# Attention of an encoder kernel: two heads at a time, scores issued alternately, transposes cut into two 64-row halves

## The chip, the core and the metric

The kernel runs on one core of one Trainium2 chip. The metric is the device time of one execution in microseconds (us). TensorE (PE) multiplies 128-row tiles and loads the stationary tile in a separate step (PEld); VectorE (DVE), ScalarE (ACT) and GpSimd (POOL) do the elementwise work; SyncE (SP) issues the transfers. PE writes to PSUM, which has eight banks; the kernel hands them out in turn.

## The reference

Two layers of an encoder over 256 tokens of width 1024, batch 1, in fp32. The change touches the attentions only:

```
q = rms_norm(...); k = rms_norm(...)          # per head, 256 tokens
s = einsum('bqhd,bkhd->bhqk', q, k) * scale   # (+ bias, + sink logit, by group)
p = softmax_f32(s)
o = einsum('bhqk,bkhv->bqhv', p, v)
```

Each layer has a first FFN, a mixer with 16 heads (8 latent heads with keys of 96 numbers; 4 windowed and 4 neighbourhood heads with keys of 64 numbers and a bias), an output projection, a cross-attention with 4 heads of 64 to 256 memory tokens, and a second FFN.

## The kernel before

Tokens lie in two tiles of 128 rows (t = 0, 1). Weights come in tiles of 128x1024, are split on ACT and DVE into a high and a low fp32r part (`whi`, `wlo`), and each product is three matmuls (`mm3`: L167, L168, L169). The FFNs are a long unbroken row of these.

A head of an attention goes through four steps. **Scores** (L438): for each t one fp32 matmul, queries stationary (64 or 96 rows, 128 columns), keys moving (256 columns); the profile shows each fp32 matmul as two passes, so a head's scores are four records. The windowed, neighbourhood and memory heads have 64-number keys: of the two heads of a `Pair`, head 0 lies in partitions 0 to 63 and head 1 in 64 to 127 of the same tile. **Softmax**: maximum on DVE (L441 for latent and memory heads, L447 with the bias for the others), exponentials on ACT (L454). **Transposes** (L465): four 128x128 blocks of the weights `p` into one PSUM bank, p stationary, an identity `ident` moving, then two copies to `pT` on DVE (L467, L468). **Values** (L474): four matmuls, `pT` stationary, V moving with 65 columns, again two passes each. When both heads of a pair are through, `finish` divides (L416, L418).

`attend` writes the heads in order: step i emits the scores of head i, the transposes of head i - d1 and the values of head i - d2. Queries and keys of the latent heads are turned one head ahead (`prep_latent`, L794, L795, 96 columns stationary, copied by ACT at L797, L798), those of the neighbourhood heads by `prep_blocks` (L739). Between the heads hooks emit other PE work: the memory keys (`mem.keys`, matmuls into `kvk`), the normed groups' transposes (L864). A scheduler then orders each engine's queue by its own estimate of times, so the written order is not kept exactly. Names: `mx0` is the mixer of layer 0, `me0` its memory attention; `sw`, `na`, `ml` are windowed, neighbourhood and latent pairs, a digit for the pair and one for the head (`mx0na01sc` holds the scores of head 1 of pair 0); `sc`, `pt`, `pv`, `qt` are the PSUM tiles of scores, turned weights, values and turned queries and keys.

## Time and profile before

| | |
|---|---|
| median of three runs | 1053.08 us (1052.95 to 1059.89) |
| the profiled execution | 1048.1 us, of which its instructions span 1046.3 us |
| PE busy | 1024.0 us, 98% |
| PE loading weights | 1002.4 us, 96% |
| DVE, ACT busy | 718.0 us (69%), 556.7 us (53%) |
| granted clock of PE | 0.996 of its upper level of 2.4 GHz |

Matmuls overlap in the profile, since each record holds the latency of its end: the time that a matmul takes from its neighbours is the distance between starts, not its duration. The two mixers' attentions lie at about 236 to 288 us and 752 to 805 us, the two memory attentions at about 321 to 332 us and 837 to 848 us.

### The profile page before, as it was taken

To read this page: it belongs to the slowest core of one execution; us is meant where nothing else is said; L and a number is where in the kernel's file an instruction comes from. 1 tells how busy PE (TensorE), PEld (TensorE's weight loads), DVE (VectorE), ACT (ScalarE), POOL (GpSimd) and SP (SyncE) were. 2 spreads that over 40 slices of the span, in tenths; PEclk is the share of its full clock that TensorE was granted. 3 is DMA by queue.
4 is the path that set the end of the run, shared out by engine and by line. 5 is a ranking of instruction groups with operands and counts; after the bars stand their busy time and mean duration, and the time that the engine had idled before them with its cause. 6 is when DMAs were issued, how large, how long until landed. Compare 5 with 4: busy or idle time off the path is not lost.

```text
span 1046.3 us, 20916 instructions
## 1 busy us (share of the span) xinstructions
PE 1024.0 (98%) x8480; PEld 1002.4 (96%) x8480; DVE 718.0 (69%) x1249; ACT 556.7 (53%) x928; POOL 114.2 (11%) x107
## 2 busy tenths in 40 slices
PE   8999999999999999999999999999999999999996
PEld 7999999998998999999999999999889999999996
DVE  7866667778786676666757666667886777766652
ACT  5755455566563565555545444546675546554541
POOL 4000000072031400000000000002600313000000
PEclk9999999999999999999999999999999999999998
DMA  8866666655042655555555555655531517666641
GB/s 277 276 208 192 198 199 206 186 173 182 22 136 67 234 189 199 188 199 192 192 184 187 188 186 184 206 186 167 181 131 32 172 38 241 204 189 196 194 130 41
DMA packets 54529, 181.79 MB, mean 174 GB/s; under 512 B 6048, under 2 KB 8992, under 8 KB 54432
## 3 DMA queue, kind: packets, MB, share of 16 engines
q1 hardware_dynamic: 54432, 180.45, 54.2%
q8 instruction: 66, 1.08, 0.4%
q14 instruction: 31, 0.25, 0.1%
HBM read 179.38 MB, written 1.05 MB: 172 GB/s over the span
## 4 chain that ended last, share of the span: by engine, by line
PE 72%; issue 17%; DVE 4%; POOL 2%; DMA 2%; ACT 2%; SPq 0%; POOLq 0%; DVEq 0%; ACTq 0%
PE f11i L169 4%; PE f11i L167 4%; PE f11i L168 4%; PE f01i L169 3%; PE f01i L167 3%; PE f01i L168 3%; PE f02i L168 3%; PE f02i L167 3%; PE f02i L169 3%; PE f11o L169 2%; PE f11o L167 2%; PE f11o L168 2%; PE f02o L169 2%; PE f01o L169 2%; PE f02o L168 2%
## 5 line engine op out<-in xcount | busy, mean ns | idle before, releaser
L141 DVE TENSOR_TENSOR wlo<-raw,whi 128x1024 fp32r<-128x1024 f32 (+4 forms) x337 | 407.5, 1214 | 208.9 <-ACT whi L140 207.7
L140 ACT CAST whi<-raw 128x1024 fp32r<-128x1024 f32 (+4 forms) x337 | 343.8, 1024 | 345.1 <-issue 86.0
L167 PE MATMUL f11i<-n10h,whi 128*128 128x256 f32 x320 | 90.1, 282 | 0.0
L168 PE MATMUL f11i<-n10l,whi 128*128 128x256 f32 x320 | 89.8, 281 | 0.0
L169 PE MATMUL f11i<-n10h,wlo 128*128 128x256 f32 x320 | 89.8, 281 | 0.0
L167 PE MATMUL f02i<-n20h,whi 128*128 128x256 f32 x320 | 88.5, 277 | 0.0
L167 PE MATMUL f01i<-n0h,whi 128*128 128x256 f32 x320 | 88.5, 277 | 0.0
L167 PE MATMUL f12i<-n21h,whi 128*128 128x256 f32 x320 | 88.5, 277 | 0.0
L169 PE MATMUL f01i<-n0h,wlo 128*128 128x256 f32 x320 | 88.4, 276 | 0.0
L168 PE MATMUL f02i<-n20l,whi 128*128 128x256 f32 x320 | 88.3, 276 | 0.0
L168 PE MATMUL f12i<-n21l,whi 128*128 128x256 f32 x320 | 88.3, 276 | 0.0
L169 PE MATMUL f02i<-n20h,wlo 128*128 128x256 f32 x320 | 88.3, 276 | 0.0
L168 PE MATMUL f01i<-n0l,whi 128*128 128x256 f32 x320 | 88.3, 276 | 0.0
L169 PE MATMUL f12i<-n21h,wlo 128*128 128x256 f32 x320 | 88.3, 276 | 0.0
L168 PEld LDWEIGHTS f11i<-n10l,whi 128*128 128x128 f32 x320 | 61.4, 192 | 0.0
L168 PEld LDWEIGHTS f12i<-n21l,whi 128*128 128x128 f32 x320 | 60.1, 188 | 0.0
L168 PEld LDWEIGHTS f02i<-n20l,whi 128*128 128x128 f32 x320 | 60.1, 188 | 0.0
L168 PEld LDWEIGHTS f01i<-n0l,whi 128*128 128x128 f32 x320 | 60.1, 188 | 0.0
L167 PEld LDWEIGHTS f01i<-n0h,whi 128*128 128x128 f32 x320 | 60.1, 188 | 0.0
L167 PEld LDWEIGHTS f11i<-n10h,whi 128*128 128x128 f32 x320 | 60.1, 188 | 0.0
L169 PEld LDWEIGHTS f01i<-n0h,wlo 128*128 128x128 f32 x320 | 60.1, 188 | 0.0
L167 PEld LDWEIGHTS f02i<-n20h,whi 128*128 128x128 f32 x320 | 60.1, 188 | 0.0
(1026 smaller groups left out, 2940.4 us busy)
## 6 DMA issues: line engine op xcount, KB each, us to landing
raw<-in_w SPq DMA_DIRECT2D x311, 512.0 KB, 4.2
raw<-in_w SPq DMA_DIRECT2D x12, 384.0 KB, 3.7
raw<-in_w SPq DMA_DIRECT2D x8, 416.0 KB, 3.3
kv0mt<-in_mem SPq DMA_DIRECT2D x8, 128.0 KB, 4.3
kv1mt<-in_mem SPq DMA_DIRECT2D x8, 128.0 KB, 3.7
gx<-in_gx SPq DMA_DIRECT2D x3, 256.0 KB, 7.2
out<-gx SPq DMA_DIRECT2D x3, 256.0 KB, 2.8
gx<-in_gx SPq DMA_DIRECT2D x1, 323.0 KB, 3.2
```

Of the source, the lines that this page charges most:

```text
L140: ins = nc.scalar.copy(hi[:, a:b], r[:, a:b])
L141: nc.vector.tensor_tensor(lo[:, a:b], r[:, a:b], hi[:, a:b].bitcast(F32), ALU.subtract)
L167: nc.tensor.matmul(ps, ah, bh, start=first, stop=False)
L168: nc.tensor.matmul(ps, ah, bl, start=False, stop=False)
L169: return nc.tensor.matmul(ps, al, bh, start=False, stop=last)
```

## The change

`attend` now steps over pairs: step i turns the latent queries of the next pair, emits the scores of pair i with the two heads alternating over t, the values of pair i - 2, a hook, and the transposes of pair i - 1. Every transpose that goes through the new `turn` (weights of all heads, queries and keys of the latent and memory heads, memory keys) is cut: rows 0 to 63 of the source go to one PSUM bank and rows 64 to 127 to another, with a 64x64 corner of the identity moving, so that one 128-row transpose becomes two with 64 moving columns. The copies out of PSUM take 64 columns of four blocks each; their number and size stay. The biased scores are written in place into `p`. The hooks stand in a new order.

```
-AT = dict(
-    d1=3, d2=5, look=3, norm1=9, turn1=11, norm2=12, turn2=14, turn0=20,
-    keys=2, ksteps=3, knorm=3, kturn=13, v0=0, v1=13, e1=2, e2=4, wturn0=7, wturn1=6,
-)
+AT = dict(look=3, turn0=20, v0=0, v1=13, wturn1=6)
...
+    halves = (slice(0, 64), slice(64, 128))
+
+    def turn(nm, blocks):
+
+
+        n = int(np.prod(blocks[0].shape[1:]))
+        ps = [acc(f"{nm}{i}") for i in range(2)]
+        for b, src in enumerate(blocks):
+            for q, r in zip(ps, halves):
+                state["turned"] = nc.tensor.transpose(q[0:n, 64 * b : 64 * b + 64], src[r], ident[r, r])
+        return ps
+
     class Pair:
 
 
-        def __init__(self, nm, o, cols):
-            self.nm, self.o, self.cols = nm, o, cols
-            self.pv, self.es = None, [None, None]
-
-        def out(self, c):
-            if self.pv is None:
-                self.pv = acc(self.nm + "pv")[:, 0:260].rearrange("p (t c d) -> p t c d", t=2, c=2)
-            return self.pv[:, :, c, :]
+
+        def __init__(self, nm, o, cols, heads):
+            self.nm, self.o, self.cols, self.heads = nm, o, cols, heads
+            self.es = [None, None]
+            for c, h in enumerate(heads):
+                h.pair, h.c, h.nm = self, c, f"{nm}{c}"
+
+        def scores(self):
+            for h in self.heads:
+                h.sc = acc(h.nm + "sc").rearrange("p (t k) -> p t k", t=2)
+            for t in range(2):
+                for h in self.heads:
+                    nc.tensor.matmul(h.sc[:, t, :], h.qT[:, t * P : (t + 1) * P], h.kT, start=True, stop=True)
+            for h in self.heads:
+                h.weights()
+
+        def transposes(self):
+            ps = turn(self.nm + "pt", [
+                h.p[:, t, kt * P : (kt + 1) * P] for h in self.heads for kt in range(2) for t in range(2)
+            ])
+            for c, h in enumerate(self.heads):
+                h.pT = tp.tile([P, 2, T], F32, tag="b2", bufs=8, name=h.nm + "pT")
+                for i, r in enumerate(halves):
+                    nc.vector.tensor_copy(
+                        h.pT.rearrange("p k (t u) -> p (k t) u", t=2)[:, :, r],
+                        ps[i][:, c * T : (c + 1) * T].rearrange("p (k u) -> p k u", k=4),
+                    )
+
+        def values(self):
+            self.pv = acc(self.nm + "pv")[:, 0:260].rearrange("p (t c d) -> p t c d", t=2, c=2)
+            for h in self.heads:
+                for t in range(2):
+                    for kt in range(2):
+                        nc.tensor.matmul(
+                            self.pv[:, t, h.c, :], h.pT[:, kt, t * P : (t + 1) * P], h.V[:, kt, h.vh, :],
+                            start=kt == 0, stop=kt == 1,
+                        )
+            self.finish()
...
-                src = tp.tile([P, 2, T], F32, tag="b2", bufs=8, name=nm + "sb")
+                src = self.p
...
-        def transposes(self):
-            ps = acc(self.nm + "pt")
-            for kt in range(2):
-                for t in range(2):
-                    o = (kt * 2 + t) * P
-                    nc.tensor.transpose(ps[:, o : o + P], self.p[:, t, kt * P : (kt + 1) * P], ident)
-            self.pT = tp.tile([P, 2, T], F32, tag="b2", bufs=8, name=self.nm + "pT")
-            nc.vector.tensor_copy(self.pT[:, 0, :], ps[:, 0:T])
-            nc.vector.tensor_copy(self.pT[:, 1, :], ps[:, T : 2 * T])
-
-        def values(self):
-            pv = self.pair.out(self.c)
-            for t in range(2):
-                for kt in range(2):
-                    nc.tensor.matmul(
-                        pv[:, t, :], self.pT[:, kt, t * P : (t + 1) * P], self.V[:, kt, self.vh, :],
-                        start=kt == 0, stop=kt == 1,
-                    )
-            if self.c == 1:
-                self.pair.finish()
-
-    def attend(heads, hooks={}, d1=AT["d1"], d2=AT["d2"]):
-
-        n = len(heads)
-        heads[0].prep()
-        for i in range(n + d2):
-            if i + 1 < n:
-                heads[i + 1].prep()
+    def attend(pairs, preps={}, hooks={}):
+
+        n = len(pairs)
+        for i in range(n + 2):
+            if i in preps:
+                preps[i]()
             if i < n:
-                heads[i].scores()
-                if i + 3 < n:
-                    heads[i + 3].load()
-            if 0 <= i - d1 < n:
-                heads[i - d1].transposes()
-            if 0 <= i - d2 < n:
-                heads[i - d2].values()
-            for h in hooks.get(i, ()):
+                pairs[i].scores()
+                for p in pairs[i + 1 : i + 3]:
+                    for h in p.heads:
+                        if h not in loaded:
+                            loaded.append(h)
+                            h.load()
+            if i >= 2:
+                pairs[i - 2].values()
+            for h in hooks.get((i, 0), ()):
                 h()
+            if 1 <= i <= n:
+                pairs[i - 1].transposes()
+            for h in hooks.get((i, 1), ()):
+                h()
+
+    loaded = []
...
-            pt = acc(self.nm + "pt")
-            for b in range(2):
-                for t in range(2):
-                    o = (b * 2 + t) * P
-                    nc.tensor.transpose(pt[:, o : o + P], self.kn[:, t, 2 * b : 2 * b + 2, :], ident)
+            ps = turn(self.nm + "pt", [self.kn[:, t, 2 * b : 2 * b + 2, :] for b in range(2) for t in range(2)])
...
-        def prep_latent(h):
+        def prep_latent(pr):
+
             if not big:
                 big["q"] = slot([P, 8, T], F32, nm + "qT")
                 big["k"] = slot([P, 8, T], F32, nm + "kT")
-            ps = acc(f"{nm}qt{h}")
-            for t in range(2):
-                nc.tensor.transpose(ps[0:96, t * P : (t + 1) * P], qn[:, t, h, :], ident)
-                nc.tensor.transpose(ps[0:96, T + t * P : T + (t + 1) * P], kn[:, t, h, :], ident)
-            q, k = big["q"][0:96, h, :], big["k"][0:96, h, :]
-            nc.scalar.activation(q, ps[0:96, 0:T], AF.Copy, scale=gq[0:96, 0:1])
-            nc.scalar.activation(k, ps[0:96, T : 2 * T], AF.Copy, scale=gn[0:96, l, G_HEAD + 1 : G_HEAD + 2])
-            heads[8 + h].qT, heads[8 + h].kT = q, k
+            hs = slice(2 * pr, 2 * pr + 2)
+            ps = turn(f"{nm}qt{pr}", [
+                a[:, t, h, :] for a in (qn, kn) for h in (2 * pr, 2 * pr + 1) for t in range(2)
+            ])
+            for i, r in enumerate(halves):
+                for a, (b, g_) in enumerate((("q", gq[0:96, 0:1]), ("k", gn[0:96, l, G_HEAD + 1 : G_HEAD + 2]))):
+                    nc.scalar.activation(
+                        big[b][0:96, hs, :].rearrange("p h (t u) -> p (h t) u", t=2)[:, :, r],
+                        ps[i][0:96, a * T : (a + 1) * T].rearrange("p (k u) -> p k u", k=4), AF.Copy, scale=g_,
+                    )
+            for h in (2 * pr, 2 * pr + 1):
+                latent[h].qT, latent[h].kT = big["q"][0:96, h, :], big["k"][0:96, h, :]
...
+        preps = {1: lambda: prep_blocks(3, 5), 2: lambda: prep_blocks(4, 6)}
+        for pr in range(4):
+            preps[3 + pr] = lambda pr=pr: prep_latent(pr)
+        attend(pairs, preps, {
+            (0, 0): [lambda: mem.keys(4)], (1, 0): [lambda: mem.keys(6)], (2, 0): [lambda: mem.keys(3)],
+            (3, 0): [lambda: mem.keys(3), mem.keys_normed], (6, 1): [mem.keys_transposed],
+            (4, 0): [lambda: group_norm(1)], (5, 1): [lambda: group_transposed(1)],
+            (6, 0): [lambda: group_norm(2)], (7, 1): [lambda: group_transposed(2)],
+        })
...
-        heads = []
-        for b in range(2):
-            pair = Pair(f"{nm}a{b}", o, [2 * b, 2 * b + 1])
-            for c in range(2):
-                s = slice(64 * c, 64 * c + 64)
-                heads.append(Head(pair, c, qT[s, b, :], memkT[s, b, :], memV, 2 * b + c))
+        pairs = [
+            Pair(f"{nm}a{b}", o, [2 * b, 2 * b + 1], [
+                Head(qT[r, b, :], memkT[r, b, :], memV, 2 * b + c) for c, r in enumerate(halves)
+            ])
+            for b in range(2)
+        ]
         oh = tp.tile([P, 2, T], F32R, tag="b2", bufs=8, name=nm + "oh")
...
-        attend(heads, {AT["wturn0"]: [lambda: out_transposed(0)]}, AT["e1"], AT["e2"])
+        attend(pairs, {}, {(2, 1): [lambda: out_transposed(0)]})
```

On PE in the mixer of layer 0, the end of the first windowed pair's transposes and the scores of the first neighbourhood pair; before:

```order
L465 MATMUL mx0sw00pt<-ident,mx0sw00p 128x128 x4
L438 MATMUL mx0na00sc<-mx0sT 128x256 x2
L465 MATMUL mx0sw01pt<-ident,mx0sw01p 128x128 x4
L167 MATMUL kv0kvk_3197<-whi_2985,kv0h 128x256
L168 MATMUL kv0kvk_3197<-wlo_2986,kv0h 128x256
L169 MATMUL kv0kvk_3197<-whi_2985,kv0l 128x256
L739 MATMUL mx0st_3201<-ident,mx0qk 128x128 x4
L438 MATMUL mx0na01sc<-mx0sT 128x256 x2
```

The same place in the changed kernel (3172 and 3173 are the two banks of the halves):

```order
L401 MATMUL mx0sw0pt_3172<-ident,mx0sw01p 128x64
L401 MATMUL mx0sw0pt_3173<-ident,mx0sw01p 128x64
L419 MATMUL mx0na00sc<-mx0sT 128x256
L419 MATMUL mx0na01sc<-mx0sT 128x256
L419 MATMUL mx0na00sc<-mx0sT 128x256
L419 MATMUL mx0na01sc<-mx0sT 128x256
L164 MATMUL kv0kvk_3165<-whi_2985,kv0h 128x256
```

The two heads' scores now stand next to each other, and directly behind 64-row transposes.

On PE in the same mixer, the transposes of the first latent pair; before, those of its head 1:

```order
L438 MATMUL mx0ml20sc<-mx0kT,mx0qT 128x256 x2
L474 MATMUL mx0na1pv<-mx0V,mx0na11pT 128x65
L465 MATMUL mx0ml01pt<-ident,mx0ml01p 128x128 x4
L474 MATMUL mx0na1pv<-mx0V,mx0na11pT 128x65 x3
L794 MATMUL mx0qt_3514<-ident,mx0qn 96x128
```

After:

```order
L440 MATMUL mx0na1pv<-mx0V,mx0na10pT 128x65 x4
L401 MATMUL mx0ml0pt_3516<-ident,mx0ml00p 128x64 x4
L401 MATMUL mx0ml0pt_3516<-ident,mx0ml01p 128x64 x3
L401 MATMUL mx0ml0pt_3517<-ident,mx0ml00p 128x64
L440 MATMUL mx0na1pv<-mx0V,mx0na11pT 128x65 x4
L401 MATMUL mx0ml0pt_3517<-ident,mx0ml00p 128x64 x3
L401 MATMUL mx0ml0pt_3517<-ident,mx0ml01p 128x64 x3
L401 MATMUL mx0ml0pt_3516<-ident,mx0ml01p 128x64
L401 MATMUL mx0ml0pt_3517<-ident,mx0ml01p 128x64
L875 MATMUL mx0ot_3542<-ident,mx0o 128x128
```

Here seven halves of the lower rows stand in a row, then a 128-row values product, then seven of the upper rows.

On DVE in the memory attention of layer 0, from the last maximum on; before:

```order
L441 TENSOR_REDUCE me0a11ng<-me0a11sc 128x2
L467 COPY me0a00pT<-me0a00pt 128x256
L468 COPY me0a00pT<-me0a00pt 128x256
L467 COPY me0a01pT<-me0a01pt 128x256
L468 COPY me0a01pT<-me0a01pt 128x256
L467 COPY me0a10pT<-me0a10pt 128x256
L468 COPY me0a10pT<-me0a10pt 128x256
L467 COPY me0a11pT<-me0a11pt 128x256
L468 COPY me0a11pT<-me0a11pt 128x256
L416 RECIPROCAL me0a0rc<-me0a0pv 128x4
```

After:

```order
L476 TENSOR_REDUCE me0a11ng<-me0a11sc 128x2
L430 COPY me0a00pT<-me0a0pt_4285 128x4x64
L430 COPY me0a00pT<-me0a0pt_4286 128x4x64
L430 COPY me0a01pT<-me0a0pt_4285 128x4x64
L430 COPY me0a01pT<-me0a0pt_4286 128x4x64
L455 RECIPROCAL me0a0rc<-me0a0pv 128x4
L457 TENSOR_TENSOR me0o<-me0a0pv,me0a0rc 128x2x64 x2
L430 COPY me0a10pT<-me0a1pt_4322 128x4x64
L430 COPY me0a10pT<-me0a1pt_4323 128x4x64
```

The division of pair 0, which needs its values from PE, now stands ahead of pair 1's copies.

## Rows read from the trace of the kernel before

**Rows 1.** The page, busy time of PE: time, share of the span, instructions.
```profile
PE 1024.0 (98%) x8480; PEld 1002.4 (96%) x8480; DVE 718.0 (69%) x1249; ACT 556.7 (53%) x928; POOL 114.2 (11%) x107
```

**Rows 2.** Stretches: length, busy time of each engine, granted clock, DMA.
```profile
236.00:288.00 52.00, 51.47 (x395) 46.84 (x394) 41.16 (x136) 32.06 (x80) 6.19 (x6) 1.00 0.31 102
321.00:332.00 11.00, 10.05 (x76) 8.63 (x76) 7.41 (x20) 3.99 (x10) 0.00 (x0) 1.00 0.00 1
752.00:805.00 53.00, 53.00 (x405) 48.35 (x404) 42.04 (x136) 33.57 (x81) 4.47 (x6) 1.00 0.26 85
```

**Rows 3.** Timeline of PE, a 64-row head alone: start us, duration us, what.
```profile
246.33 0.60 PE L739 MATMUL mx0st<-ident,mx0qk 128*128 128x128 f32 x4
246.86 1.13 PE L438 MATMUL mx0na01sc<-mx0sT 64*128 64x256 f32 x4
247.92 0.39 PE L167 MATMUL kv0kvk<-whi,kv0h 128*128 128x256 f32 x1
248.15 0.28 PE L168 MATMUL kv0kvk<-wlo,kv0h 128*128 128x256 f32 x1
```

**Rows 4.** Timeline of PE, a head's values; a 96-row head and what follows.
```profile
252.25 1.00 PE L474 MATMUL mx0sw0pv<-mx0V,mx0sw01pT 128*128 128x65 f32 x8
...
260.32 1.03 PE L438 MATMUL mx0ml01sc<-mx0kT,mx0qT 96*128 96x256 f32 x4
261.18 0.60 PE L465 MATMUL mx0na10pt<-ident,mx0na10p 128*128 128x128 f32 x4
```

**Rows 5.** Timeline of PE, three 64-row heads in a row.
```profile
236.29 0.48 PE L438 MATMUL mx0sw00sc<-mx0sT 64*128 64x256 f32 x1
236.31 0.48 PE L438 MATMUL mx0sw01sc<-mx0sT 64*128 64x256 f32 x1
236.61 0.38 PE L438 MATMUL mx0sw00sc<-mx0sT 64*128 64x256 f32 x1
236.63 0.38 PE L438 MATMUL mx0sw01sc<-mx0sT 64*128 64x256 f32 x1
...
237.26 1.02 PE L438 MATMUL mx0sw10sc<-mx0sT 64*128 64x256 f32 x4
238.22 0.61 PE L251 MATMUL kv0ps<-cmean,kv0s 128*128 128x1 f32 x4
```

**Rows 6.** Timeline of PE's weight loads at the same place.
```profile
236.29 0.18 PEld L438 LDWEIGHTS mx0sw00sc<-mx0sT 64*128 64x128 f32 x1 [0.25 <-issue]
236.31 0.18 PEld L438 LDWEIGHTS mx0sw01sc<-mx0sT 64*128 64x128 f32 x1
236.40 0.19 PEld L438 LDWEIGHTS mx0sw00sc<-mx0sT 64*128 64x128 f32 x1
```

**Rows 7.** Lines L739, L794, L474: duration ns min/median/max, first and last start, forms.
```profile
L739 PE MATMUL mx0st<-ident,mx0qk x8: 270/272/273, 239.8 to 246.7; 128*128 128x128 f32 x8
L739 PEld LDWEIGHTS mx0st<-ident,mx0qk x6: 138/140/140, 239.9 to 246.6; 128*128 128x128 f32 x6
...
L794 PEld LDWEIGHTS mx0qt<-ident,mx0qn x2: 123/124/125, 257.2 to 257.4; 128*96 128x96 f32 x2
...
L474 PEld LDWEIGHTS mx0sw0pv<-mx0V,mx0sw00pT x8: 188/192/192, 249.6 to 250.4; 128*128 128x128 f32 x8
L474 PE MATMUL mx0sw0pv<-mx0V,mx0sw00pT x8: 219/275/275, 249.8 to 250.5; 128*128 128x65 f32 x8
```

**Rows 8.** Timelines of DVE, ACT and PE in the memory attention of layer 0.
```profile
322.43 0.69 DVE L441 TENSOR_REDUCE me0a00ng<-me0a00sc 128x2 f32<-128x512 f32 x1 [1.07 <-PE me0a01sc L438]
325.71 0.41 DVE L467 COPY me0a00pT<-me0a00pt 128x256 f32<-128x256 f32 x1
328.89 0.49 DVE L418 TENSOR_TENSOR me0o<-me0a0pv,me0a0rc 128x128 f32<-128x128 f32 x2
...
323.15 0.84 ACT L454 ACTIVATE me0a00p<-me0a00sc,me0a00ng 128x256 f32<-128x256 f32 x2 [1.31 <-DVE me0a00ng L441]
...
331.10 0.97 PE L167 MATMUL me0wo<-me0oh,whi 128*128 128x256 f32 x6 [0.52 <-ACT me0oh L931]
```

89 lines of the change are left out of this document (33 added, 56 removed).

## Prediction, made before the changed kernel had run

> **What bounds the kernel now.** I read the busy times first: PE is busy for 1024.0 of 1046.3 us [rows 1], so time is won only where PE's queue gets shorter or a gap in it closes. The stretches come next: in the mixers' attentions PE is busy almost throughout, 51.47 of 52.00 us in layer 0, while DVE has 41.16 and ACT 32.06; the memory attention is 11.00 us with 10.05 busy [rows 2]. So the mixers' attentions are priced by starts on PE, the memory attentions by a chain through DVE and ACT. The rest of the kernel keeps its order and costs nothing here. The change reaches about 52 + 53 + 2 x 11 = 127 us; one per cent of the total would be 8% of that.
>
> **Part A: scores side by side.** A 96-row head starts at 260.32 and what follows at 261.18: four passes in 0.86 us, 0.215 each [rows 4]. At the start of the mixer the order put three 64-row heads in a row. There the records of heads 0 and 1 start 0.02 us apart and advance together, 0.22 per round, and the third head starts at 237.26: two heads in the time of one [rows 5]. So two heads in different halves of the rows run at the same time when they stand together. Before, that holds for the first windowed pair and the first memory pair only. After, by the order, it holds also for the second windowed and first neighbourhood pair of each layer and the second neighbourhood pair of layer 1 (in layer 0 two matmuls of memory keys stand between its heads): five mixer pairs, 5 x 0.86 = **-4.3 us**. The latent heads have 96 rows; alternating them changes nothing.
>
> **Part B: going to 64 rows and back.** A 64-row head alone costs more than its passes. The transposes ahead have 0.109 between starts ((0.60 - 0.272)/3 [rows 3, 7]), so theirs end at 246.77; the scores start at 246.86, a gap of 0.09. The next row starts 1.06 later, 0.20 more than the 0.86 of a 96-row head. That row lasts 0.39 where the next one of its kind lasts 0.28: another 0.11, a load that nothing hid [rows 3, 4]. Together 0.40 us for each excursion into 64 rows. The three heads in a row show the same once for all: 1.93 us between 236.29 and 238.22, against two rounds of 0.86 [rows 5]. Now every turned tile is 64-row work among 128-row work. Counting stretches of 64-row work in the two orders: the mixers have 12 before, 37 after (19 and 18), since keys, values and latent scores stand between, and some tiles are cut into two or three stretches. For transposes I take 0.36, the load at the entry being shorter (Part C): 37 x 0.36 - 12 x 0.40 = **+8.5 us**. This is no longer hidden anywhere: PE waits for itself.
>
> **Part C: the halves.** A block of 128 rows costs 0.109 now. Its matmul lasts 272 ns with 128 moving columns; the values' lasts 219 with 65 (the shortest): 0.84 ns a column, so 64 columns are 0.054 us. Its load lasts 140 ns with 128 columns and 124 with 96, about 0.5 ns a column: 0.064 us or less for 128 [rows 7]. The loads of two heads in different halves of the rows start together too: 236.29 and 236.31, the second one of head 0 already at 236.40 [rows 6]. So a pair of halves, running side by side, should take about 0.060 in place of 0.109. The two mixers have 2 x (64 weights + 32 queries and keys + 4 memory keys) = 200 blocks: 200 x 0.049 = -9.8. But the order puts halves of one bank in a row and a values product between them in the first three latent pairs: 14, 13 and 10 slots of 0.060 where 8 would do, 2 x 13 x 0.060 = +1.6. Sum **-8.2 us**.
>
> The Trainium skill speaks against this part: "TensorE: Matmul & The Clock Gate", section "LDWEIGHTS (loading the stationary operand)", gives a load as columns over 1.2 GHz, whatever the rows. By that a half would load as long as a whole block, 0.107 us, and Part C would give nothing. The rows contradict it for transposes: their loads are 52 ns shorter than the 192 of the values' loads with the same 128 columns.
>
> **Part D: new waits in the mixers.** Pairs are coarser than heads, but between a pair's scores and its transposes there lies a whole step, some 7 us of PE, against 0.69 + 0.84 us a head on DVE and ACT. The narrow place is the end: the values of the third latent pair follow its transposes after four output transposes, while DVE has first to finish pair 1 and then make two copies of 0.41 [rows 8]. I estimate 0.95 us a layer, **+1.9 us**; bounds 0 (DVE is early) and 4. The copies and activations keep count and size.
>
> **Part E: memory attention.** From the first maximum at 322.43 to the output projection at 331.10 are 8.67 us [rows 8]. After: four maxima end at 2.5 us after the first; the copies of pair 0 end at 3.9; values of its head 0 run from 3.3 to 4.4, pair 1's halves to 5.0, values of head 1 to 6.0. Then DVE divides (about 0.8 us) before it copies pair 1, since the order puts that first; its four copies end at 8.1, the values at 9.3. The shorter scores and transposes are lost in this chain: +0.7 a layer, and 0.15 for the turned queries: **+1.7 us**, bounds -2 (the chain stays, PE's saving counts) and +4.
>
> **Sum.** -4.3 + 8.5 - 8.2 + 1.9 + 1.7 = -0.4 us on the profiled execution's 1048.1 us. The median of the runs is 5 us above that execution, with the same program, so I apply the difference to the median: 1052.7, rounded **1053 us**. What is gained by going side by side is paid again for changing over.
>
> **The rivals.**
> 1. *A half costs as much as a block, but the two go side by side.* The values' passes start (1.00 - 0.275)/7 = 0.104 apart with only 65 moving columns [rows 4, 7]: loads, not columns, pace them. If the halves are paced like that, the 200 blocks save nothing and the slots in a row cost 2 x 13 x 0.105 = 2.7: -0.4 + 8.2 + 2.7 = +10.5, 1064. Against it: the 140 ns loads. This is also the time to which the skill's rule on loads leads.
> 2. *Slower: PE paces every load and matmul one after another, at 0.105.* No row shows a longer run of starts closer than about 0.104; the 0.02 in [rows 5] may come from instructions that had waited together. Then a pair of halves costs 0.21, 200 x (0.21 - 0.109) = +20, and some 3 us in the memory chains: 1053 + 8 + 20 + 3 = 1084. It decides from 0.11 us a pair on: there the sum passes +10.5. The skill (same page, section "Wait — 56ns, not 53.3ns?") names 62 ns a matmul for one way of decoding; by that a pair would cost 0.124 and the sum be about 1064.
> 3. *Faster: the change-over is cheaper for transposes.* If only the gap and load at the entry count, 0.09 + 0.06 = 0.15, then 35 excursions cost 7 us less: 1046. If the memory chain also keeps PE's saving, 1042.
> 4. *The change does not do what it says.* Partly seen in the order already (the second neighbourhood pair of layer 0, the halves in rows) and in the sum. If halves of one bank are in fact run beside later ones of the other, this gives back 1.6.
>
> **How the numbers follow.** A measurement of this kernel can tell about 1% (10.5 us) from no change. The forecast, 1046 to 1060, has 0.60; rival 1 0.15, half of it over the bound; rival 2 0.09, all slower; rival 3 0.16, mostly within 1%, as its 1046 is. So faster 0.14 (rival 3 with a cheap memory chain, and what I may have priced too high in B), same 0.67, slower 0.19. The range reaches from rival 3's lower end to rival 1: 1042 to 1065; outside are rival 2 and a little on each side.
>
> **What would show it.** Part A: records of `na00sc` and `na01sc` start 0.02 apart, the pair in about 0.9 us. Part B: about 0.1 us between the last start of 128-row work plus its pitch and the first half, and a long first matmul behind. Part C: sixteen halves of one tile in about 0.5 us; 0.9 is rival 1, 1.7 rival 2. Part D: a wait of PE for copies ahead of `mx0ml2pv`. Part E: output projection 9.3 us after the first maximum. The forecast is wrong if the halves of a tile take over 0.9 us, if PE waits over 4 us a layer, or if the excursions cost under 0.2.

## The result: slower by 3%, and the profile after

The changed kernel takes 1096.21 us (median of four executions, 1083.37 to 1111.22) beside 1053.49 (1052.95 to 1059.89): a ratio of 1.0306, 95% interval 1.0214 to 1.0398. Every ratio here leaves out slow runs, those over 1.5% above the fastest of their kernel, so this one compares the two shorter executions, 1083.37 and 1091.08 us, with the four of before. The prediction was 1053, and its range ended at 1065. The profiled execution is the longest of those measured, with a mean granted clock of 0.944; in the others it was 0.947 to 0.965, so all four lost the clock for long (before: 0.996).

The page of the changed kernel: PE's busy time, and the granted clock of PE in 40 slices of 27.7 us, in tenths.

```profile
PE 1080.9 (97%) x8720; PEld 1046.9 (94%) x8720; DVE 717.6 (65%) x1249; ACT 558.5 (50%) x930; POOL 115.6 (10%) x107
PEclk9999999997599999999999999999856979999998
```

DVE, ACT and POOL do what they did [rows 1]; PE is busy 56.9 us longer. The clock row has a dent in each layer's mixer and a smaller one behind the second, in the memory attention of layer 1. The stretches of the changed kernel show the first two sharply: length, busy time of PE, PEld, DVE, ACT and POOL, then the granted clock, DMA share and GB/s.

```profile
236.00:261.50 25.50, 22.95 (x218) 18.84 (x219) 22.32 (x80) 16.74 (x37) 4.33 (x4) 1.00 0.68 208
261.50:305.50 44.00, 44.00 (x248) 38.69 (x248) 18.32 (x53) 13.88 (x38) 1.39 (x2) 0.50 0.00 1
305.50:342.00 36.50, 35.34 (x304) 34.48 (x304) 25.66 (x44) 20.20 (x38) 11.80 (x10) 1.00 0.44 145
...
794.00:852.00 58.00, 58.00 (x321) 50.87 (x322) 24.34 (x80) 17.45 (x47) 3.03 (x3) 0.50 0.03 12
852.00:887.00 35.00, 33.84 (x291) 32.98 (x291) 25.48 (x44) 20.02 (x38) 11.80 (x10) 1.00 0.50 150
```

Before, both mixers ran at 1.00 [rows 2], which is 2.4 GHz. Now PE runs at 0.50, 1.2 GHz, for 44 us in layer 0 and 58 us in layer 1, busy all the time. The first matmuls of the output projection stand ahead of the return in both layers, by 2.8 and 4.2 us. By an estimate, what takes 44 us at half the clock takes 22 at the full one: that is about the +21.6 us by which the mixer of layer 0 has grown (85.0 to 106.6, from the first windowed scores to the first memory scores); 58 gives 29, the mixer of layer 1 grew by 28.0. The memory attentions add 1.3 and 6.7 (the second one partly at 0.50). Of the 63.1 us that the span has grown, 57.6 are these four stretches; 5.4 more are in the last feed-forward, whose input matmuls take 281 ns where they took 276. That is not the change's: in the kernel before, another feed-forward (`f11i`) had 281 and now has 277.

What stands ahead of the falls, in the changed kernel's timeline of PE (start, duration, what, idle time before it and what ended it):

```profile
244.41 0.43 PE L419 MATMUL mx0na00sc<-mx0sT 64*128 64x256 f32 x1
244.41 0.43 PE L419 MATMUL mx0na01sc<-mx0sT 64*128 64x256 f32 x1
...
245.42 0.39 PE L164 MATMUL kv0kvk<-whi,kv0h 128*128 128x256 f32 x1
...
250.37 0.41 PE L401 MATMUL mx0sw1pt<-ident,mx0sw11p 64*128 64x64 f32 x8
250.62 0.39 PE L401 MATMUL mx0qt<-ident,mx0qn 64*96 64x64 f32 x8
250.84 0.39 PE L401 MATMUL mx0qt<-ident,mx0kn 64*96 64x64 f32 x8
...
260.76 1.43 PE L440 MATMUL mx0na0pv<-mx0V,mx0na00pT 128*128 128x65 f32 x8 [1.40 <-DVE mx0na00pT L430]
...
265.07 0.66 PE L401 MATMUL mx0qt<-ident,mx0qn 64*96 64x64 f32 x8
265.52 0.64 PE L401 MATMUL mx0qt<-ident,mx0kn 64*96 64x64 f32 x8
266.09 1.22 PE L419 MATMUL mx0ml10sc<-mx0kT,mx0qT 96*128 96x256 f32 x2
...
793.91 2.04 PE L419 MATMUL mx1na11sc<-mx1sT 64*128 64x256 f32 x4 [1.90 <-DVE mx1sw11pT L430]
```

Until the fall the work goes by as it was priced: two heads' scores start together and the next work follows 1.01 us later; eight halves go by in 0.22 to 0.25. Then PE waits 1.40 us for DVE's copies, to 260.76 (1.90 in layer 1, to 793.91). The clock falls between 261.0 and 261.5 (in layer 1 between 793.5 and 794.0), and eight halves take 0.45. Why DVE was late in layer 0, from its timeline:

```profile
257.62 0.49 DVE L457 TENSOR_TENSOR mx0o<-mx0sw1pv,mx0sw1rc 128x128 f32<-128x128 f32 x2
259.20 0.75 DVE L619 TENSOR_TENSOR kv0kn<-kv0kvk,kv0f 128x256 f32<-128x256 f32 x2 [1.09 <-POOL kv0f L170]
259.87 0.74 DVE L430 COPY mx0na00pT<-mx0na0pt 128x256 f32<-128x256 f32 x2
```

The scaling of the memory keys waits 1.09 us for GpSimd, and the copies for PE's values are queued behind it. In layer 1 two weight splits of 1.22 us stand there.

### The profile page after: what moved, and what is told of

The parts are those of the page before. It is cut to its first block, busy times and chain, and to the rows that moved or that the text cites. A ratio compares the mean times of both kernels' runs of the same rounds, so it can differ in the third digit from the quotient of the medians.

```text
span 1109.4 us, 21392 instructions
## 1 busy us (share of the span) xinstructions
PE 1080.9 (97%) x8720; PEld 1046.9 (94%) x8720; DVE 717.6 (65%) x1249; ACT 558.5 (50%) x930; POOL 115.6 (10%) x107
## 4 chain that ended last, share of the span: by engine, by line
PE 66%; issue 18%; DVE 7%; DMA 3%; POOL 3%; ACT 2%; SPq 0%; POOLq 0%; DVEq 0%; ACTq 0%
PE f01i L165 3%; PE f11i L165 3%; PE f11i L166 3%; PE f11i L164 3%; PE f01i L164 3%; PE f01i L166 3%; PE f02i L166 3%; PE f02i L164 3%; PE f02i L165 3%; DVE wlo L138 2%; DMA raw<-in_w 2%; PE f02o L166 2%; PE f02o L164 2%; PE f02o L165 2%; PE f11o L166 2%
## 5 line engine op out<-in xcount | busy, mean ns | idle before, releaser
L166 PEld LDWEIGHTS f12i<-n21h,wlo 128*128 128x128 f32 x320 | 61.4, 192 | 0.0
L164 PEld LDWEIGHTS f12i<-n21h,whi 128*128 128x128 f32 x320 | 60.1, 188 | 0.0
```

Of the source, the lines that this page charges most:

```text
L164: nc.tensor.matmul(ps, ah, bh, start=first, stop=False)
L166: return nc.tensor.matmul(ps, al, bh, start=False, stop=last)
```

## The experiments

Two questions: what lets the clock fall, and what holds it at 0.50. For all kernels of the encoder, from their timelines in us, one profiled execution each (mixer: first windowed scores to first memory scores; memory: from there to the second feed-forward; time at 0.50 within the mixer's attention, read in windows of 0.5 us):

| kernel | mixer 0, 1 | memory 0, 1 | at 0.50 in mixer 0, 1 |
|---|---|---|---|
| before | 85.0, 83.9 | 15.9, 15.9 | 0, 0 |
| changed | 106.6, 111.9 | 17.2, 22.6 | 44, 58 |
| e1 pairs, whole transposes | 84.5, 84.5 | 16.3, 16.3 | 0, 0 |
| e2 heads, halves | 89.7, 86.4 | 16.2, 16.2 | 0, 0 |
| e4 before, pauses | 93.2, 85.3 | 15.9, 15.9 | 10.5, 0 |
| e6 changed, waits away | 83.8, 83.5 | 22.7, 21.2 | 0, 0 |
| e7 heads, halves, pauses | 109.0, 101.9 | 20.6, 16.2 | 44.5, 34.5 |
| e10 e6, old memory steps | 83.5, 83.4 | 15.9, 15.9 | 0, 0 |
| e11 pairs, whole, pauses | 93.5, 84.7 | 16.3, 16.3 | 14, 0 |
| e12 pairs, whole, waits away | 83.0, 82.5 | 15.9, 15.9 | 0, 0 |
| e13 changed, halves in runs, pauses | 107.1, 102.9 | 22.6, 17.2 | 44, 30.5 and 3.5 |
| e14 changed, halves cut up, pauses | 101.5, 114.4 | 21.2, 21.1 | 30.5, 61.5 |
| e16 latent heads whole, pauses | 92.2, 91.7 | 17.2, 22.6 | 7, 3.5 |
| e17 weights whole, pauses | 92.5, 91.0 | 16.3, 16.3 | 10, 10.5 |

**One part undone: whole transposes in steps by pairs (e1).**

```diff
-        ps = [acc(f"{nm}{i}") for i in range(2)]
+        ps = [acc(f"{nm}{i}") for i in range(len(blocks) // 4)]
         for b, src in enumerate(blocks):
-            for q, r in zip(ps, halves):
-                state["turned"] = nc.tensor.transpose(q[0:n, 64 * b : 64 * b + 64], src[r], ident[r, r])
+            q, o = ps[b // 4], (b % 4) * P
+            state["turned"] = nc.tensor.transpose(q[0:n, o : o + P], src, ident)
...
```

> The changed kernel with one part undone: pair steps and the heads' scores side by side stay, but each transpose is again one of 128 rows, four to a bank. Theory 1 (a pause): the clock falls because the steps by pairs are coarser, so that PE stands still for 1 to 2 us waiting for DVE's copies, and attention work at 1.2 GHz does not bring it back before the output projection. Then the waits are still here, the granted clock falls to 0.5 in at least one mixer, and the time is 1070 to 1110 us. Theory 2 (the halves): the 64-row transposes themselves let the clock fall. Then it stays at 1.00 in both mixers, and the time is 1049 to 1058 us. Theory 3 (the scores side by side): as theory 1, without a wait of over 1 us ahead of the fall.

Measured: 1052.48 us beside 1048.17, ratio 1.0024 (0.9989 to 1.0058), as theory 2 has it. Both mixers, with the output projection:

```profile
235.00:320.00 85.00, 82.56 (x668) 77.57 (x667) 65.79 (x176) 51.23 (x115) 18.33 (x16) 1.00 0.38 125
...
750.00:835.00 85.00, 82.42 (x665) 77.24 (x663) 65.23 (x173) 51.29 (x115) 15.12 (x14) 1.00 0.36 115
```

The clock stays at 1.00, with 1.00 and 1.01 us as the longest waits where the changed kernel waited 1.40 and 1.90. So the time is lost with the halves, and neither by pairs as such nor by scores side by side. Whether it is their form or the longer waits that came with them, this run can't tell.

**One part alone: halves in steps by heads (e2).**

```diff
-            ps = acc(self.nm + "pt")
-            for kt in range(2):
-                for t in range(2):
-                    o = (kt * 2 + t) * P
-                    nc.tensor.transpose(ps[:, o : o + P], self.p[:, t, kt * P : (kt + 1) * P], ident)
+            ps = turn(self.nm + "pt", [self.p[:, t, kt * P : (kt + 1) * P] for kt in range(2) for t in range(2)])
...
```

> The kernel before with one part of the change alone: transposes in halves of 64 rows into two banks (the latent heads' for two heads at a time), while steps stay by single heads and their scores are not alternated. Theory 1 (a pause): PE's waits stay under 0.7 us, the clock stays at 1.00 in the mixers, and the time is 1048 to 1060 us (the price of more excursions into 64-row work against 8 us from the shorter transposes). Theory 2 (the halves): the clock falls to 0.5 in both mixers without a wait of over 1 us ahead of it, and the time is 1070 to 1115 us. Theory 3 (scores side by side): 1048 to 1060 us at 1.00.

Measured: 1058.81 to 1097.76 us in four executions; the two shorter give a ratio of 1.0121 (1.0015 to 1.0227), too uncertain to call. The profiled execution is the shortest; its mixers stay at 1.00 and are still 4.7 and 2.5 us longer than before. Their 39 excursions into 64-row work where there were 12 would fit that, but it is not shown. The other executions took 10, 27 and 39 us longer, at mean granted clocks of 0.990, 0.963 and 0.951 beside 0.993: in the two longest the clock was low for long, but no trace shows behind which waits. So theory 2, a fall without a wait of over 1 us, did not come true in the profiled execution, and these two executions leave it open.

**A pause put into the kernel before (e4).** `tc.issue_after(x)` puts what is written under it behind the instruction x.

```diff
+        with tc.issue_after(behind.ins):
+            g = nc.tensor.matmul(a[0:16, 0:16], z, nhalf, start=True, stop=True)
+        nc.gpsimd.tensor_tensor(z[:, 0:w], cmean[:, 0:1].to_broadcast([P, w]), nhalf[:, 0:w], ALU.pow)
+        with tc.issue_after(g.ins):
+            return nc.tensor.matmul(b[0:16, 0:16], z, nhalf, start=True, stop=True)
...
+            if gap and i == gap[0]:
+                rest.enter_context(tc.issue_after(pause(gap[1], state["turned"]).ins))
...
+        attend(heads, hooks, gap=(9, 16 if l == 0 else 2))
```

> The kernel before with nothing of the change, and one pause of PE put into each mixer ahead of its tenth attention step (PE waits for one GpSimd power of 16 columns, about 3 us, in layer 0, and of 2 columns, about 1 us, in layer 1). Theory 1: in layer 0 the clock falls to 0.5 behind the pause and stays there to the output projection, which makes that mixer 20 to 35 us longer; in layer 1 it falls or not, by which side of its bound 1 us lies: 1075 to 1090 us in all, or 1095 to 1115 if both fall. Theories 2 and 3: the clock stays at 1.00, and the time is 1053 plus the pauses, 1056 to 1060 us.

Measured: 1051.58 us, ratio 1.0002 (0.9963 to 1.0040). The stretches around the pause of layer 0:

```profile
262.00:272.50 10.50, 9.21 (x38) 8.18 (x39) 3.44 (x10) 3.40 (x10) 1.93 (x2) 0.51 0.10 41
272.50:290.00 17.50, 17.50 (x146) 16.73 (x144) 13.87 (x42) 11.24 (x29) 0.70 (x1) 1.00 0.01 1
```

The clock falls in a wait of 3.47 us; one of 0.83 in layer 1 is not followed by a fall. So far theory 1 holds, and theories 2 and 3 do not. But theory 1's time is missed, since the attention with whole transposes brings the clock back after 10.5 us, not the output projection after 40: the mixer grew by 8.3, pause included. In all ten executions the mean granted clock was 0.988 to 0.994, where the changed kernel had 0.944 to 0.965. A fall alone does not make the loss; something in the changed kernel holds it.

**Bare phases (e3).** No encoder: stretches of one kind of matmul.

> No encoder: a program that leaves out all of the computation and runs stretches of matmuls on loaded data, each of 20 to 30 us and each followed by 240 dense fp32r matmuls of 128x256: whole fp32 transposes; halves in two banks; 64-row scores one by one; the same in two row groups side by side; values of 65 columns; the mix of a mixer step with whole transposes; the same with halves; then these mixes, values, and fp32r matmuls with a pause of PE put in that waits for DVE (about 1 and about 2 us). Theory 1: the stretches without a pause stay at a granted clock of 1.00, the halves too; those with a pause of 2 us fall to 0.5 behind it and stay there to the end of the stretch, with the fp32r matmuls bringing it back. Theory 2: halves and the mix with halves fall to 0.5 without a pause, whole transposes don't. Theory 3: the scores side by side fall, the others don't.

Measured: granted clock 1.00 from end to end. The pauses failed, since other matmuls were ordered into them and PE stood still for 0.3 us at most. What it shows: in these stretches 64-row work alone, halves included, did not let the clock fall.

**Phases with pauses that nothing fills (e5).**

```diff
+        with tc.issue_after(g.ins):
+            last = nc.tensor.matmul(banks[7][:, 0:128], z[:, 0:P], x[:, 1, 0:128], start=True, stop=True)
+        rest.close()
+        rest.enter_context(tc.issue_after(last.ins))
```

> No encoder again: it leaves out all of the computation and runs stretches of matmuls on loaded data, each with one pause of PE in it that nothing can fill (PE waits for one, two or three DVE operations of 1.2 us), and 200 dense fp32r matmuls of 128x256 behind each stretch. Theory C (a pause lowers the clock, and what follows decides when it comes back): behind the pauses of about 3 and 4 us the granted clock falls to 0.5; in the mix with whole transposes it is back at 1.00 within 15 us, in the mix with halves it stays at 0.5 to the end of the stretch, 40 us or more; the pause of about 1.7 us is on the border. Theory H (halves alone): the stretches with halves fall ahead of the pause, those with whole transposes don't fall. Theory P (the pause alone, and its length decides how long the clock is low): both mixes come back after the same time. The pure stretches (values, whole transposes, halves, scores of 64 rows alone and side by side, scores of 96 rows) say by which kind of work it comes back; open, no forecast but that the fp32r matmuls bring it back.

PE's waits were 1.64, 2.90 and 4.16 us. Behind 1.64 no fall, behind the others always. Both mixes were back at 1.00 after 3.5 to 7 us, with halves as with whole transposes, so theories C and H both failed here. The pure stretches differ, as rows of PE's timeline show:

```profile
651.33 106.77 PE L80 MATMUL bank<-x 128*128 128x65 f32 x500
...
801.97 29.59 PE L60 MATMUL bank<-ident,x 128*128 128x128 f32 x250
...
870.81 26.92 PE L66 MATMUL bank<-ident,x 64*128 64x64 f32 x800
...
944.68 51.56 PE L75 MATMUL bank<-x 64*128 64x256 f32 x120
...
1036.64 28.73 PE L71 MATMUL bank<-x 64*128 64x256 f32 x240
```

500 passes of values took 0.214 each, all at 0.50, and the clock came back only in the fp32r matmuls behind them; so with 64-row scores one by one (0.43 a pass, 58 us at 0.50). With whole transposes, halves, scores side by side, scores of 96 rows and fp32r it was back 3.5 to 7 us after it fell. So here it was the work behind a pause that decided whether the clock returned.

**The waits taken away from the changed kernel (e6).** DVE's queue is put in another order; the output projection is held behind the last copies.

```diff
+            (3, 1): [behind(mem.keys_scaled), more(2)],
...
+            (4, 0): [lambda: group_norm(1)], (4, 1): [more(3)], (5, 1): [lambda: group_transposed(1)],
...
+        with tc.issue_after(state["pT"].ins):
+            project(nm, "mo", mo_order(), 8, oT["h"], oT["l"], nn, {AT["turn0"]: lambda: group_transposed(0)})
```

> The changed kernel with DVE's queue put in another order: the scaling of the memory keys and two weight splits (1.2 us each) of the output projection go behind the copies of the third and fourth pair's transposes, and the other splits of that projection behind the last copies. Halves, pair steps and alternated scores are all kept. Theory C: the two waits of PE (1.40 and 1.90 us) go down to under 1.1, the clock stays at 1.00 in both mixers in the profiled execution, the mixers take 80 to 85 us each instead of 107 and 112, and the time is 1038 to 1060 us. Theory H: the clock falls all the same, 1075 to 1110 us.

Measured: 1058.80 us, ratio 1.0079 (1.0044 to 1.0113). Mixer of layer 0 in two stretches, then its memory attention:

```profile
235.00:281.00 46.00, 45.49 (x460) 39.87 (x459) 37.47 (x127) 30.39 (x76) 5.61 (x6) 1.00 0.23 70
281.00:319.00 38.00, 36.77 (x313) 35.83 (x311) 29.57 (x51) 20.27 (x38) 10.89 (x10) 1.00 0.58 194
319.00:342.00 23.00, 20.65 (x136) 18.60 (x136) 9.63 (x27) 5.52 (x14) 0.00 (x0) 0.70 0.01 2
```

With 0.74 us as the longest wait of PE in the mixers, the clock stays, and the mixers are 1.2 and 0.5 us shorter than before (DVE's new order has a part in that; see e12). Theory H fails: in the mixers the waits were what let the clock fall. The loss that is left sits in the memory attentions (+6.8 and +5.3), which fall behind waits of 0.42 and 0.84 us; behind the same two waits in layer 0 of the changed kernel the clock had stayed.

**Halves by heads, with the pauses (e7).** The edit of the second and the third experiment together.

> The kernel with halves by single heads and the same two pauses as in the kernel before with pauses (about 3.5 us in layer 0, 0.8 us in layer 1). Theory C: in layer 0 the clock falls behind the pause and is at 0.5 until the output projection, 30 us or more, instead of the 11 us with whole transposes; in layer 1 it does not fall: 1075 to 1095 us. Theory P: it is back after 11 us as with whole transposes, 1055 to 1070 us.

Measured: 1100.83 us. Layer 0, from the fall to the return:

```profile
257.00:301.50 44.50, 41.29 (x234) 32.56 (x232) 17.96 (x58) 16.95 (x47) 5.92 (x4) 0.50 0.06 19
```

10.5 us with whole transposes, 44.5 with halves, and the clock was back 6 us ahead of the output projection. The fall came at 257.0 already, behind a wait of 0.55 us and ahead of the pause; in layer 1 it came with the pause, here 1.68 us long, and lasted 34.5. So theory P fails: in this kernel the halves keep the clock down longer. Theory C's time (1075 to 1095) is missed, since layer 1 fell too.

**Whole transposes by pairs, with the pauses (e11).** The edit of the first and the third together.

> The kernel with whole transposes and steps by pairs, with the pause of about 3.5 us in layer 0 and 0.8 us in layer 1 at the same place as in the kernel before with pauses. Theory C2 (halves hold the clock down): it falls at the pause of layer 0 and is back at 1.00 within 15 us, as by single heads with whole transposes: 1050 to 1062 us. Rival (the steps by pairs hold it down, since values then come 8 in a row): it stays at 0.5 for 30 us or more, to the output projection: 1070 to 1085 us.

Measured: 1053.55 us; 14 us at 0.50 from a pause of 3.03 us on, none behind 0.83. It is not the steps by pairs that hold it:

```profile
265.00:279.00 14.00, 12.61 (x54) 11.68 (x55) 4.88 (x14) 4.15 (x10) 2.00 (x2) 0.51 0.01 1
279.00:291.00 12.00, 12.00 (x99) 11.58 (x96) 9.28 (x27) 7.53 (x21) 0.69 (x1) 1.00 0.00 1
```

**Phases in the kernel's order (e8).** Steps by pairs, and by heads:

```diff
+            values(8)
+            if fr:
+                dense(fr)
+            turn(8)
+            turn(8)
+            alone(4, 96)
...
+            values(4)
+            turn(4)
+            alone(2, 96)
+            turn(4)
```

> No encoder: all of its computation is left out. Matmuls on loaded data in the order and numbers of the latent steps, 8 values, 8 and 8 transposes, 4 scores of 96 rows (steps by pairs), or half of each at a time (steps by heads), with whole transposes or halves; in each stretch one pause of PE (4.2 us, in the last four stretches 2.9 us), values first behind it, and 200 dense fp32r matmuls behind the stretch. Theory C2 (behind a pause the clock comes back only when little of what follows is values work, and halves take the whole transposes' share of PE's time away): with whole transposes the clock is back at 1.00 within 15 us by pairs and by heads; with halves it stays at 0.5 to the end of the stretch, over 40 us, by pairs and by heads; with 8 fp32r matmuls put into each pair step it comes back although there are halves. Theory D (it is the kernel's other waits and changes of mode that hold the clock down, not the kind of work): all stretches are back within 15 us, those with halves too, as in the phases before.

By pairs whole 7 us at 0.50, by heads whole 6.5 or none, by heads halves 75, twice, to the fp32r matmuls: as C2 has it. But by pairs halves came back after 6.5 and 17 us (with fp32r matmuls put in 10), so C2 does not explain the changed kernel, which steps by pairs. One stretch of halves by heads, and one by pairs:

```profile
327.00:402.00 75.00, 73.95 (x402) 57.38 (x403) 0.99 (x1) 0.00 (x0) 0.00 (x0) 0.51 0.00 1
...
628.50:645.50 17.00, 16.38 (x110) 14.93 (x111) 0.56 (x1) 0.00 (x0) 0.00 (x0) 0.51 0.00 1
```

**Halves in runs, and cut up (e13, e14).** In the changed kernel some values stand between the halves of a pair. Two kernels, pauses in both layers: in the first the halves stand in runs, behind all values of the pair ahead; in the second values of one head, 8 halves, values of the other head and 8 halves follow each other.

```diff
+            if 2 <= i <= n and gap:
+                with tc.issue_after(state["pv"].ins):
+                    pairs[i - 1].transposes()
```

```diff
+            if 2 <= i <= n and gap:
+                cut(pairs[i - 2], pairs[i - 1])
```

> The changed kernel with a pause of PE of about 3.5 us in both mixers (ahead of the sixth step) and a fixed order: the halves of a pair go behind all values of the pair ahead of it, so that 16 halves of weights, 16 of latent heads and 4 scores stand in a row. Theory R (an uninterrupted run of halves and scores brings the clock back, as in the phases in the kernel's order; values in between keep it down): the clock falls at each pause and is back at 1.00 within 15 us, and each mixer takes 90 to 97 us; in all 1065 to 1085 us. Rival (something else of the kernel holds it down): it stays at 0.5 for 30 us or more to the output projection in both, mixers of 105 us or more, 1090 to 1115 us in all.

> As the kernel with halves in runs, pauses included, but with the values of one head put between the two heads' halves, so that halves come 8 at a time between values. Theory R: the clock falls at each pause and stays at 0.5 for 30 us or more, mixers of 105 us or more, 1090 to 1120 us in all. Rival: the same as with halves in runs, whichever that is.

Measured: 1096.60 and 1098.79 us. In runs 44 and 30.5 us at 0.50, cut up 30.5 and 61.5; these are the low stretches, first two in runs, then two cut up:

```profile
263.00:307.00 44.00, 39.58 (x241) 35.13 (x237) 17.54 (x50) 12.79 (x36) 4.25 (x3) 0.50 0.00 1
795.50:826.00 30.50, 27.47 (x174) 23.66 (x173) 13.61 (x48) 10.27 (x28) 5.19 (x3) 0.50 0.05 18
...
254.50:285.00 30.50, 27.40 (x170) 22.75 (x169) 12.62 (x40) 10.45 (x28) 5.23 (x3) 0.50 0.13 40
787.00:848.50 61.50, 58.47 (x327) 49.98 (x328) 24.88 (x79) 17.78 (x48) 5.92 (x4) 0.50 0.04 11
```

Theory R failed: in neither order was it back within 15 us. (Falls came ahead of the pauses put in: behind 1.40 and 1.90 us of waiting in runs, behind 1.12 and two of 0.73 and 0.46 cut up. So all four low stretches hold a pause of 3.03 us as well.) The rival's "to the output projection" holds in two of the four only: both stretches of 30.5 us ended 14 and 15 us ahead of it. In runs the clock fell a second time in layer 1, behind 1.18 us of waiting, and was back after 3.5 us, with the projection's first matmuls.

**Phases with zeros (e15).** The values and half of the transposes take zeros in place of data.

> No encoder: all of its computation is left out. The pair steps in the kernel's order again (8 values, 8 and 8 transposes, 4 scores of 96 rows) with one pause in each stretch and 200 fp32r matmuls behind it; some stretches take zeros in place of data for the values and for half of the transposes, as softmax weights are mostly near zero. Halves on data, halves with zeros, whole with zeros, each twice behind a pause of 4.2 us, and halves on data and with zeros behind 2.9 us. Theory Z (what the matmuls multiply decides): halves with zeros stay at 0.5 for over 30 us, halves on data come back within 15 us as before. Rival: the data make no difference, all come back within 15 us; if stretches alike differ among themselves by more than 15 us, the time of the return is no fixed function of the work.

Halves on data 7, 27 and 13.5 us at 0.50; with zeros 24, 6.5 and 6.5; whole with zeros 10.5 and 7. Stretches that are alike differ by 20 us with halves on data, by 17 with halves on zeros, by 3.5 with whole transposes. Above that scatter no difference between data and zeros shows: theory Z failed, and the rival's last clause came true, that the time of the return is no fixed function of the work.

**Which halves (e16, e17).** Pauses in both layers, and only the latent heads' or only the weights' transposes whole.

```diff
-            ps = turn(f"{nm}qt{pr}", [
+            ps = whole(f"{nm}qt{pr}", [
```

```diff
-            ps = turn(self.nm + "pt", [
+            ps = whole(self.nm + "pt", [
```

> The changed kernel with the pause of about 3.0 us ahead of the sixth step in both mixers, and the latent heads' transposes whole; the weights' stay in halves. Theory S (the share of halves sets how late the clock comes back): between whole (11 to 14 us) and halves (30 to 60 us) in both mixers, 15 to 35 us, 1070 to 1095 us in all. Rival (only one kind matters): 11 to 14 us here and over 30 us with the weights whole, or the other way round.

> The same with the weights' transposes whole and the latent heads' in halves. Theory S: 15 to 35 us, 1070 to 1095 us in all. Rival: over 30 us where the other is at 11 to 14, or the other way round.

Measured: 1065.61 and 1058.43 us. First with the latent heads whole, then with the weights whole, the low stretch of layer 0:

```profile
263.50:270.50 7.00, 3.97 (x19) 3.40 (x19) 2.57 (x10) 2.05 (x6) 3.56 (x2) 0.51 0.01 2
```

```profile
266.50:276.50 10.00, 10.00 (x52) 9.14 (x51) 3.59 (x10) 3.23 (x8) 0.43 (x1) 0.50 0.01 2
```

3.5 to 10.5 us in four mixers, as with all transposes whole. Neither theory S nor its rival has this: in these four mixers, one execution of each kernel, either kind could be in halves, and only both together kept the clock low for 30 us and more.

**A version with the best of both (e10, e12).** The changed mixers without the waits and the old memory steps (by heads, whole); and the same with whole transposes by pairs in the mixers.

```diff
-        attend(pairs, {}, {(2, 1): [lambda: out_transposed(0)]})
+        by_heads([h for p in pairs for h in p.heads], lambda: out_transposed(0))
```

> The changed kernel with the waits taken away, and in the memory attention alone the old steps: single heads, whole transposes. The mixers with the waits taken away took 1.2 and 0.4 us less than before the change, the memory attention 6.8 and 5.3 more, most of it at 0.5 of the clock. Theory C: the memory attention is back at 15.9 us a layer at 1.00, and the time is 1.5 us under that of the kernel before, 1043 to 1054 us beside 1048 to 1054. Rival: the clock falls in the memory attention all the same, because it does so behind any mixer with halves: 1053 to 1062 us.

> Steps by pairs and scores side by side in the mixers with whole transposes, with DVE's queue put in order as in the kernel with the waits taken away, and the memory attention as before the change. If the wait of 1.0 us a mixer ahead of the fourth pair's values goes: mixers 83.5 us instead of 84.6, the clock at 1.00 throughout, and 1.5 to 2.5 us under the kernel before: 1044 to 1054 us. Rival: DVE's splits only move to where they delay something else: as the kernel with whole transposes by pairs, 1047 to 1056 us.

Measured: 1049.12 us, ratio 0.9992 (0.9963 to 1.0022), and 1049.22, ratio 0.9976 (0.9945 to 1.0007). The memory attention is back at 15.9 us in both layers, as theory C has it. The first kernel's mixer and memory attention of layer 0, then its mixer of layer 1:

```profile
236.00:281.00 45.00, 44.49 (x453) 38.85 (x451) 36.37 (x126) 30.45 (x76) 5.71 (x6) 1.00 0.23 72
...
320.00:336.00 16.00, 15.05 (x119) 13.77 (x118) 9.74 (x27) 5.51 (x14) 0.00 (x0) 1.00 0.00 2
752.00:796.00 44.00, 43.49 (x447) 38.12 (x443) 35.24 (x122) 29.63 (x75) 3.03 (x3) 1.00 0.18 55
```

In all ten executions of the first its mean granted clock was 0.992 to 0.997, with all of the change but its waits in the mixers. No gain over the kernel before is proven for either. The second one's mixers are 1.9 and 1.4 us shorter than before, and 1.5 and 2.0 shorter than those of e1, which have DVE's old order; the first one's, with halves, are 0.4 and 0.9 us longer than the second one's.

## Why the prediction was wrong

**The step that failed** is in no part by itself: every duration was read in stretches at a granted clock of 1.00 [rows 2] and taken over as if the change could not move the clock. Part D then priced a wait at its own length, 0 to 4 us. The waits were 2.5 us in layer 0 up to the fall (0.59, 0.34, 0.17 and 1.40) and 2.4 in layer 1 (0.52 and 1.90), beside 0.95 a layer; 3 us more than the sum has. What follows them costs 50: the two mixers grew by 21.6 and 28.0. None of the rivals names the clock. Rival 2 gives 1084, near the measured time, by luck: its mechanism is not there, as halves go by at 0.03 us, not 0.105.

**Shown**: that both mixers ran at 0.50 for 44 and 58 us, which is the loss; that the waits let it fall, since the same kernel without them keeps 1.00 (e6, e10); and that the halves keep it there longer. With both kinds in halves the clock was low for 30.5 to 61.5 us in eight mixers, with one kind or none for 3.5 to 14 in six, although the waits at those falls were mostly longer (3.0 to 3.5 us). The comparison is not quite like for like: five of the eight had a pause inside the low stretch. The three that had none (the changed kernel, and layer 1 of e7) were low for 34.5 to 58 us. Nor do halves bar the return: in four of the eight it came 6 to 15 us ahead of the output projection, among halves. The Trainium skill, "TensorE: Matmul & The Clock Gate", section "HAM oscillation — how this bites in real kernels", says that waits between PE's bursts throttle its clock; the rows agree that a wait of PE stands at each fall in the mixers, here of 0.55 to 3.5 us. The same page of the Trainium skill, section "What's actually happening", says that activity releases it; here PE was busy for 44.00 of 44.00 us at 0.50, so a busy PE is not enough.

**Still open**: which property of the halves does it. In the kernel it is not the steps by pairs (e11), nor whether halves stand in runs or cut up (e13, e14). In bare phases the order did matter: halves by heads were low for 75 us in both stretches (e8), halves by pairs for 6.5 to 27 us in eight, on data as with zeros (e8, e15). So the changed kernel, which steps by pairs, adds something that these phases lack. Which wait is long enough is open too: a fall came behind 0.55 us in e7, none behind 1.00 in e1, 0.98 in e2 or 1.64 in e5. That halves make the fall easier would fit the first two and the two long executions of e2, but is not shown.

**Part A** was right in its mechanism: two heads start together, 1.01 us for the pair. But the second neighbourhood pair of layer 1 was counted wrongly: its heads follow each other (790.93 and 793.91), so four pairs gain and not five, -3.4 us for -4.3. **Part B** and **Part C** were right, and rivals 1 and 3 wrong; PE's queue has the 37 excursions counted. PE's rows of the kernel with the waits taken away, at 1.00:

```profile
257.41 1.06 PE L440 MATMUL mx0na0pv<-mx0V,mx0na01pT 128*128 128x65 f32 x8
258.40 0.46 PE L401 MATMUL mx0na1pt<-ident,mx0na10p 64*128 64x64 f32 x8
258.70 0.42 PE L401 MATMUL mx0na1pt<-ident,mx0na11p 64*128 64x64 f32 x8
258.95 0.39 PE L401 MATMUL mx0qt<-ident,mx0qn 64*96 64x64 f32 x8
259.17 0.39 PE L401 MATMUL mx0qt<-ident,mx0kn 64*96 64x64 f32 x8
259.49 0.70 PE L419 MATMUL mx0ml10sc<-mx0kT,mx0qT 96*128 96x256 f32 x2
260.02 0.60 PE L419 MATMUL mx0ml11sc<-mx0kT,mx0qT 96*128 96x256 f32 x2
260.46 0.59 PE L419 MATMUL mx0ml10sc<-mx0kT,mx0qT 96*128 96x256 f32 x2
...
276.66 1.08 PE L440 MATMUL mx0ml2pv<-mx0V,mx0ml20pT 128*128 128x65 f32 x8 [0.51 <-ACT mx0oh L173]
```

Eight passes of values at 0.104 end at 258.24, the halves start 0.16 later; the last eight end at 259.41, the scores start 0.08 later, and their first two passes take 0.53 to the next where the following take 0.44. That is 0.33 us for the excursion, beside 0.36 forecast. The 32 halves, 16 blocks, take 1.01 us: 0.063 a block beside 0.060 forecast and 0.109 before [rows 3, 7]. **Part D**'s wait ahead of `mx0ml2pv` is there with 0.51 us for 0.95, and it is ACT's copy that ends it. Together A to D were -2.1 us for the two mixers; without the long waits they measure -1.7 (e6) and -2.1 (e10). That agreement is in part luck, since DVE's new order alone is worth 3.5 us with whole transposes (e1 against e12). **Part E** put 0.85 us on each memory attention; layer 0 has +1.3 at 1.00, but behind the projection's start, not ahead: that comes 8.74 us after the first maximum, not 9.3. In layer 1 the clock decides, +6.7.

```profile
343.60 0.69 DVE L476 TENSOR_REDUCE me0a00ng<-me0a00sc 128x2 f32<-128x512 f32 x1 [1.80 <-PE me0a01sc L419]
...
352.34 0.84 PE L164 MATMUL me0wo<-me0oh,whi 128*128 128x256 f32 x5
```

So at the upper clock the change is worth about nothing, as the sum says, and it made the kernel one in which a wait of 1.40 us was followed by 44 us at half speed and one of 1.90 us by 58.

## What to carry to other kernels

Ahead of a change to PE's work, look for what may make PE wait anew, and ask what the work behind the wait does to the granted clock: here a wait was not priced by its length. Where shorter PE instructions only win what going over to 64 rows and back costs again, the longer ones are the safer choice: with whole transposes the clock was back after 14 us at most in every kernel and bare phase here.

## What the runs showed of the hardware that was not expected

- Behind a pause, values of 128x65 in fp32 ran at 0.50 for 106.77 us, and 64-row scores one by one for 51.56, with PE busy all the time; the same scores in two row groups side by side were back at 1.00 after 7 us.
- Stretches of halves that are alike, behind the same pause of 4.16 us, were low for 7 and for 27 us.
- 8 halves in two row groups take 0.22 to 0.25 us at 2.4 GHz and 0.45 at 1.2.
